# Recurrence score levels computed by 64-column halves of the TensorE array, with the diagonal joined to the first pair of levels

## The chip, the cores and the metric

The kernel runs on one core of a Trainium2 chip. The metric is the device time of one execution, in microseconds; three runs of the kernel before gave 2126.22 to 2127.8, with a median of 2127.6. A core has five engines that run side by side and meet by semaphores: TensorE (PE in the profile; its weight loads are PEld), VectorE (DVE), ScalarE (ACT), GpSimd (POOL) and SyncE (SP, which issues most DMAs). Matmul results go to PSUM, everything else lies in SBUF; both have 128 partitions.

## The reference, cut to what matters

Two layers of a decoder trunk on 512 tokens of width 1024. Each layer is a feed-forward block, a mixer and another feed-forward block. The mixer adds a gated linear recurrence (4 heads of 128 channels) and a sliding-window attention. The change lies in the recurrence:

```python
log_f = jnp.logaddexp(jnp.log(lb), jnp.log1p(-lb) + jax.nn.log_sigmoid(z))   # f = lb + (1-lb)*sigmoid(z)
k = (1.0 - lb) * jax.nn.sigmoid(-z)
...
G = jnp.cumsum(gb, axis=2)
o_inter = jnp.einsum('bhtd,bhde->bhte', qb * jnp.exp(G), state)
diff = G[:, :, :, None, :] - G[:, :, None, :, :]
decay = jnp.exp(jnp.where(causal[:, :, None], diff, -jnp.inf))
scores = jnp.einsum('bhtd,bhtsd,bhsd->bhts', qb, decay, kb)
o = o_inter + jnp.einsum('bhts,bhse->bhte', scores, vb)
```

In words: the score of query t and key s (s not after t) is the sum over channels of q[t] times k[s] times the product of the forget gates f of all tokens after s up to t. The output of a head is the score matrix times the values, normalised and gated. The reference does it in chunks of 64 tokens with a carried state; the kernel forms the whole 512 x 512 lower triangle of scores instead.

## The kernel before, in words

**Layout.** Activations lie with channels on the partitions and the 512 tokens along the free axis, in tiles `s` of 128 x 512 fp32 (61 slots). PSUM is cut into five tiles `acc` and three tiles `aux` of 128 x 512. Weights come by DMA (`w<-wall`, issued on SyncE), and each unit is split into two halves of its precision: ScalarE casts it to `whi` (L321) and VectorE subtracts to get `wlo` (L328); six such pairs are held, so a new cast waits until TensorE has done the last matmul with the pair six before it. Every projection is three matmuls per block (hi x hi, hi x lo, lo x hi; `mm3`), recorded at L115, the line of the helper `mm`. The recurrence uses plain fp32 matmuls, each of which shows as two records.

**Order of the work.** TensorE's program order is the order of the calls (manual schedule). The helper class `Order` keeps an estimated TensorE time `order.t`, to which each `mm` adds its estimated length. Side work (recurrence heads, attention blocks, transposes) is written as generators that yield a waiting time from the table `WAIT`; after the matmuls of each projection block `order.poll()` steps those that are due, at least `WAIT["rest"]` apart. So the side matmuls are placed between projection matmuls. The other engines' instructions are ordered by the scheduler of the framework; each engine runs its own list strictly in order.

**One head of the recurrence** is the generator `run` in `mixer`, which calls `recurrence_scores(q, f, kz, box)`. Its inputs are q, f and k (here `kz`), 128 channels x 512 tokens. The scores inside each chunk of 128 tokens (four chunks, tile `sd`) are built by levels b = 1, 2, 4, ..., 64: at level b the tokens are taken in groups of 2b, and the queries of the second half of a group meet the keys of its first half, both already multiplied with the gates between them and the middle of the group.

- `qa = q * f` (L943). The diagonal: four matmuls of 128 keys x 128 queries into an `aux` tile `p0`, then one VectorE product with the identity writes the whole of `sd` (L949), diagonal kept and all else zero.
- `meet(b)` (L984, L986, L988) multiplies the second-half queries and first-half keys of level b with the gate products, in place in `qa` and `kz`, and forms the products for the next level (`pr`).
- The levels are done in pairs (1,2), (4,8), (16,32). For a pair, a tile `mv` of 128 x 4 x 192 gathers the moving operand of each chunk: 64 query columns of level b (ScalarE, L995), 64 of level 2b (ScalarE, L998), and 64 of level 2b times one more gate (VectorE, L1000). After `WAIT["pair"]` four matmuls, one for each chunk, all 128 keys against 192 columns, go into two `aux` tiles `lv`. Two VectorE placements per group and `lv` tile (`place`, L972, a predicated copy with the constant `mask`) put the wanted entries into `sd`.
- The last level (64) is four matmuls of 128 keys x 64 queries, `meet(64)`, and two placements.
- Then the scores between chunks are made by larger matmuls (`s1`, `s2`; L1034 to L1043), and `run` multiplies all score blocks with the values.

In each layer heads 0 and 1 run first, beside the projections of keys and queries of attention; heads 2 and 3 run later, beside attention and the first branch projections. The score tiles, attention and the transposes share the three `aux` tiles.

**Existing matmuls with 64 stationary columns.** Attention's product with the values writes alternately to partitions 0 to 63 and 64 to 127 of one `aux` tile: `mm(po[e * HD : (e + 1) * HD, :], va[:, v0 : v0 + HD], pt[b, e], ...)` for e = 0, 1.

Of the kernel before, what the change touches and what calls it, by code (L numbers as in the profile page):

```python
# [29 lines left out]
SLOTS = 61  # L30

WAIT = dict(
    early=0.0, first=0.0, spread=2300.0, squares=1700.0, lay=34500.0, laid=770.0, normed=7600.0, final=2600.0,
    head=2600.0, diag=0.0, level=1720.0, chunks=1270.0, blocks=350.0, norm=2370.0, gate=8000.0,
    values=1200.0, scores=2000.0, exp=9000.0, shares=4500.0, turn=1900.0, turned=3000.0, rest=1200.0, lent=3500.0, apart=4000.0, block=2000.0, pair=4000.0, att0=1260.0, att1=12300.0,
)
W32, WS, AHEAD, TAIL, PLAIN, FIRST, EARLY, LATE = 4, 6, 3, 4, 4, 7, 4, 8
# [8 lines left out]
def trunk(ctx: ExitStack, tc: tile.TileContext, xin, wall, gains, lbT, hgain, sinks, c_dist, c_mask, c_ident, out):  # L46
# [25 lines left out]
    def aux():  # L72
        return ps.tile([P, S], F32, tag="aux", name=nm("aux"), bufs=3)
# [40 lines left out]
    def mm(o, lhsT, rhs, start, stop):  # L114
        nc.tensor.matmul(o, lhsT, rhs, start=start, stop=stop)  # L115
        n = 1
        for d in rhs.shape[1:]:
            n *= d
        order.t += max(n / 2.4, 27.0) * 4 if rhs.dtype == F32 else max(n / 2.4, 107.0)

    def transpose(o, src):
        nc.tensor.transpose(o, src, ident)  # L122
# [815 lines left out]
    def recurrence_scores(q, f, kz, box):  # L938

        qa = big()
        nc.vector.tensor_tensor(qa, q, f, op=ALU.mult)  # L943
        sd = big(F32, [P, TT, P])
        p0 = aux()
        for c in range(TT):
            cs = slice(c * P, (c + 1) * P)
            mm(p0[:, cs], kz[:, cs], q[:, cs], True, True)
        nc.vector.tensor_tensor(  # L949
            sd, p0.rearrange("p (c t) -> p c t", c=TT), ident.unsqueeze(1).to_broadcast([P, TT, P]), op=ALU.mult  # L950
        )
        yield WAIT["diag"]
        pr = big()
        prod, off = f, 0

        def halves(t, b):

            v = t.rearrange("p (n two b) -> p n two b", two=2, b=b)
            return v[:, :, 0, :], v[:, :, 1, :]

        def odd(t, b):
            return t.rearrange("p (c n two b) -> p c n two b", c=TT, two=2, b=b)[:, :, :, 1, :]

        def dense(t, b):
            return t.rearrange("p c (n b) -> p c n b", b=b)

        def spread(v, b):
            return v.to_broadcast([P, v.shape[1], b])

        def place(b, m, src, c):  # L970

            nc.vector.copy_predicated(  # L972
                sd.rearrange("p c (n two b) -> p c n two b", two=2, b=b)[:, c, :, 1, :],
                mask[:, m, :].rearrange("p (n b) -> p n b", b=b).unsqueeze(1).to_broadcast([P, 2, 64 // b, b]),
                dense(src, b),
            )

        def meet(b):

            nonlocal prod, off  # L980
            n = S // (2 * b)
            pv = prod.rearrange("p (n two) -> p n two", two=2)
            kv, qw = halves(kz, b)[0], halves(qa, b)[1]
            nc.vector.tensor_tensor(qw, qw, spread(pv[:, :, 0:1], b), op=ALU.mult)  # L984
            yield
            nc.vector.tensor_tensor(kv, kv, spread(pv[:, :, 1:2], b), op=ALU.mult)  # L986
            nxt = pr[:, off : off + n]
            nc.vector.tensor_tensor(nxt, pv[:, :, 0], pv[:, :, 1], op=ALU.mult)  # L988
            prod, off = nxt, off + n

        for i, b in enumerate(LEVELS[:-1:2]):


            mv = sb.tile([P, TT, 192], F32, tag="tt", name=nm("mv"), bufs=2)
            nc.scalar.copy(dense(mv[:, :, :64], b), odd(qa, b))  # L995
            first = meet(b)
            next(first)
            nc.scalar.copy(dense(mv[:, :, 64:128], 2 * b), odd(qa, 2 * b))  # L998
            way = prod.rearrange("p (c n four) -> p c n four", c=TT, four=4)[:, :, :, 1:2]
            nc.vector.tensor_tensor(  # L1000
                dense(mv[:, :, 128:], 2 * b), odd(qa, 2 * b), way.to_broadcast([P, TT, P // (4 * b), 2 * b]), op=ALU.mult
            )
            yield WAIT["pair"]
            lv = [aux()[:, :384].rearrange("p (c t) -> p c t", c=2) for _ in range(2)]
            for c in range(TT):
                mm(lv[c // 2][:, c % 2, :], kz[:, c * P : (c + 1) * P], mv[:, c, :], True, True)
            next(first, None)
            for _ in meet(2 * b):
                pass
            for j, v in enumerate(lv):  # L1010
                c = slice(2 * j, 2 * j + 2)
                place(b, 3 * i, v[:, :, :64], c)
                place(2 * b, 3 * i + 1, v[:, :, 64:128], c)
                place(2 * b, 3 * i + 2, v[:, :, 128:], c)
            yield WAIT["level"]
        b = LEVELS[-1]
        lv = aux()
        for c in range(TT):
            mm(lv[:, c * b : (c + 1) * b], kz[:, c * P : (c + 1) * P], qa[:, c * P + b : (c + 1) * P], True, True)
        for _ in meet(b):  # L1020
            pass
        v = lv[:, :256].rearrange("p (c t) -> p c t", c=TT)
        for j in range(2):
            c = slice(2 * j, 2 * j + 2)
            place(b, len(MASKS) - 1, v[:, c, :], c)
        yield WAIT["level"]

        s1 = big(F32, [P, 2, P])
        p1 = aux()
        for i, (s, t) in enumerate(((0, 1), (2, 3))):  # L1030
            mm(p1[:, i * P : (i + 1) * P], kz[:, s * P : (s + 1) * P], qa[:, t * P : (t + 1) * P], True, True)
        for s, t in ((0, 1), (2, 3)):
            ks, qt = kz[:, s * P : (s + 1) * P], qa[:, t * P : (t + 1) * P]
            nc.vector.tensor_scalar(ks, ks, prod[:, t : t + 1], None, op0=ALU.mult)  # L1034
            nc.vector.tensor_scalar(qt, qt, prod[:, s : s + 1], None, op0=ALU.mult)
        nc.scalar.copy(s1, p1[:, : 2 * P].rearrange("p (c t) -> p c t", c=2))
        yield WAIT["chunks"]

        s2 = big(F32, [P, 2, 2 * P])
        p2 = aux()  # L1040
        for s in range(2):
            mm(p2[:, s * 256 : (s + 1) * 256], kz[:, s * P : (s + 1) * P], qa[:, 256:512], True, True)
        nc.scalar.copy(s2, p2.rearrange("p (c t) -> p c t", c=2))  # L1043

        def block(s, t):
            if s == t:
                return sd[:, s, :]
            if (s, t) in ((0, 1), (2, 3)):
                return s1[:, s // 2, :]
            return s2[:, s, (t - 2) * P : (t - 1) * P]  # L1050

        box.append(block)
        yield WAIT["blocks"]
# [236 lines left out]
    nc.sync.dma_start(ident, c_ident)  # L1290
    dist = const([P, 256], "dist")
    nc.sync.dma_start(dist, c_dist)
    mask = const([P, len(MASKS), 64], "mask", I32)
    nc.sync.dma_start(mask, c_mask)
    lb_in = const([P, DEPTH, H], "lb_in")
    nc.sync.dma_start(lb_in, lbT)
    hgh = const([P, DEPTH, P], "hgh")
# [136 lines left out]
```

## Time and profile before

| what | value |
|---|---|
| runs, device us | 2127.6, 2126.22, 2127.8 (median 2127.6) |
| span of the profiled execution, first to last instruction | 2123.9 us (the runs' median lies 3.7 above it) |
| granted TensorE clock, mean over the span | 0.999 |
| TensorE busy | 2110.6 us |
| VectorE busy | 1573.4 us |
| ScalarE busy | 1119.0 us |
| predicated placements (L972) | 160, together 47.7 us busy |
| pair matmuls (`aux<-mv,s`) | 192 records, together 35.6 us busy |

"Busy" is the time in which an engine has at least one instruction in flight; the last figure of a group is the mean length of one. Instructions on one engine overlap at their ends, so a group's busy time divided by its count can be less than the mean length. In the lists in order of time the columns are start (us from the start of the span), length in us, engine, line, operation, output<-inputs, shapes and how many were merged into the row; what stands in brackets is idle time ahead and what ended it.

### The profile page before, as it was taken

Reading aid. Unit: us, or ns where it says so; the run is one execution under the profiler, and the core shown is the slowest. Engines: PE = TensorE matmul, PEld = TensorE weight load, DVE = VectorE, ACT = ScalarE, POOL = GpSimd, SP = SyncE. Lnnn points to the kernel's source line nnn. Section 1 sums busy time; section 2 is a strip of 40 time slices with the busy share of each in tenths; the row PEclk is TensorE's granted clock in tenths of the full one; section 3 lists DMA queues with packets and bytes.
Section 4 is the critical chain, followed back from the end, with each engine's and each line's share of the span. In section 5 each row is a group of like instructions: output and inputs, shape, how many; then the busy total and the mean of one; then the engine's idle time right before and its main releaser. Section 6 shows DMA issues by size and latency. Waiting matters only on the chain.

```text
span 2123.9 us, 34765 instructions
## 1 busy us (share of the span) xinstructions
PE 2110.6 (99%) x13293; PEld 1898.1 (89%) x13293; DVE 1573.4 (74%) x2793; ACT 1119.0 (53%) x1884; POOL 152.2 (7%) x180
## 2 busy tenths in 40 slices
PE   9999999999999999999999999999999999999998
PEld 8899988887888999998899998898778989999987
DVE  5877886768776777789587778767687757777884
ACT  7555555346445555556455556453554545555562
POOL 0011000000000011110001110000000000111000
PEclk9999999999999999999999999999999999999999
DMA  8677663221236357774447775632122463677751
GB/s 251 149 185 182 167 181 118 92 67 64 66 100 208 120 125 176 182 197 123 153 113 177 183 183 141 197 119 80 60 70 60 124 194 110 149 180 182 185 158 51
DMA packets 146870, 298.48 MB, mean 141 GB/s; under 512 B 15664, under 2 KB 73488, under 8 KB 146704
## 3 DMA queue, kind: packets, MB, share of 16 engines
q1 hardware_dynamic: 121216, 228.31, 32.7%
q0 software_dynamic: 25344, 67.91, 18.6%
q8 instruction: 104, 1.70, 0.3%
q14 instruction: 62, 0.51, 0.1%
q10 hardware_dynamic: 144, 0.05, 0.0%
HBM read 213.58 MB, written 14.73 MB: 107 GB/s over the span
## 4 chain that ended last, share of the span: by engine, by line
PE 75%; DVE 7%; ACT 3%; issue 1%; DMA 1%; SPq 0%; ACTq 0%; DVEq 0%
PE acc L115 55%; PE aux L115 19%; DVE s L398 1%; PE aux L122 1%; ACT whi L321 1%; DVE wlo L283 1%; DMA w<-wall 1%; DVE wlo L328 1%; PE acc L122 1%; ACT s L397 1%; DVE tt L265 0%; DVE w L264 0%; DVE s L273 0%; DVE w L274 0%; ACT whi L278 0%
## 5 line engine op out<-in xcount | busy, mean ns | idle before, releaser
L115 PE MATMUL acc<-s,whi 128*128 128x256 f32 (+1 forms) x4968 | 1068.8, 312 | 0.7 <-DVE s L901 0.7
L115 PEld LDWEIGHTS acc<-s,whi 128*128 128x128 f32 x4968 | 810.1, 191 | 48.7 <-issue 3.7
L115 PE MATMUL acc<-s,wlo 128*128 128x256 f32 (+1 forms) x2484 | 770.2, 310 | 0.1
L115 PEld LDWEIGHTS acc<-s,wlo 128*128 128x128 f32 x2484 | 474.1, 191 | 26.0 <-DVE wlo L328 0.4
L321 ACT CAST whi<-w 128x1024 fp32r<-128x1024 f32 (+1 forms) x341 | 316.6, 947 | 242.0 <-PE aux L115 100.2
L115 PE MATMUL acc<-whi,s 128*128 128x512 f32 x1264 | 414.5, 394 | 0.0
L321 ACT CAST whi<-tt 128x1024 fp32r<-128x1024 f32 x154 | 161.4, 1048 | 337.7 <-DVE tt L315 199.5
L328 DVE TENSOR_TENSOR wlo<-w,whi 128x1024 fp32r<-128x1024 f32 (+1 forms) x181 | 218.5, 1216 | 135.3 <-ACT whi L321 131.6
L115 PEld LDWEIGHTS acc<-whi,s 128*128 128x128 f32 x1264 | 237.1, 188 | 55.7 <-issue 3.2
L328 DVE TENSOR_TENSOR wlo<-tt,whi 128x1024 fp32r<-128x1024 f32 x154 | 188.1, 1222 | 101.6 <-ACT whi L321 101.6
L326 POOL DMA_DIRECT2D wlo<-w x160 | 138.2, 865 | 1723.5 <-ACT wlo L325 1363.1
L115 PE MATMUL acc<-wlo,s 128*128 128x512 f32 x632 | 246.7, 390 | 1.2 <-DVE wlo L283 1.2
L115 PE MATMUL aux<-s,whi 128*128 128x256 f32 x1232 | 225.1, 283 | 0.0
L115 PE MATMUL aux<-whi,s 128*128 128x512 f32 x592 | 196.7, 390 | 0.0
L115 PEld LDWEIGHTS aux<-s,whi 128*128 128x128 f32 x1232 | 192.2, 192 | 0.0
L115 PE MATMUL aux<-s,wlo 128*128 128x256 f32 x616 | 174.3, 283 | 0.0
L115 PEld LDWEIGHTS acc<-wlo,s 128*128 128x128 f32 x632 | 118.8, 188 | 25.5 <-DVE wlo L283 2.4
L115 PEld LDWEIGHTS aux<-whi,s 128*128 128x128 f32 x592 | 111.2, 188 | 22.9
L325 ACT ACTIVATE wlo<-w 128x1024 fp32r<-128x1024 f32 (+1 forms) x160 | 129.8, 844 | 0.0
L397 ACT CAST s<-s 128x512 fp32r<-128x512 f32 (+1 forms) x164 | 88.4, 580 | 75.8 <-DVE s L456 72.2
L115 PEld LDWEIGHTS aux<-s,wlo 128*128 128x128 f32 x616 | 118.3, 192 | 0.0
L115 PE MATMUL aux<-wlo,s 128*128 128x512 f32 x296 | 115.2, 389 | 0.0
(182 smaller groups left out, 2189.1 us busy)
## 6 DMA issues: line engine op xcount, KB each, us to landing
w<-wall SPq DMA_DIRECT2D x267, 512.0 KB, 3.7
wlo<-w POOLq DMA_DIRECT2D x83, 512.0 KB, 5.5
w<-wall SPq DMA_DIRECT2D x288, 128.0 KB, 3.4
wlo<-w POOLq DMA_DIRECT2D x77, 256.0 KB, 3.3
x_d<-s SPq DMA_DIRECT2D x48, 256.0 KB, 2.1
s<-x_d SPq DMA_DIRECT2D x48, 256.0 KB, 5.5
w<-wall SPq DMA_DIRECT2D x34, 256.0 KB, 3.2
s<-wall SPq DMA_DIRECT2D x64, 128.0 KB, 3.7
```

The source lines that it names most:

```text
L115: nc.tensor.matmul(o, lhsT, rhs, start=start, stop=stop)
L122: nc.tensor.transpose(o, src, ident)
L283: nc.vector.tensor_tensor(it.lo[:, h[c]], w[c], it.hi[:, h[c]].bitcast(F32), op=ALU.subtract)
L321: i = nc.scalar.copy(it.hi[:, c], w[:, c])
L325: nc.scalar.mul(it.lo[:, c], w[:, c], -1.0)
L326: nc.gpsimd.dma_start(it.lo[:, c].bitcast(F32), w[:, c], accum_op=ALU.add)
L328: nc.vector.tensor_tensor(it.lo[:, c], w[:, c], it.hi[:, c].bitcast(F32), op=ALU.subtract)
L397: nc.scalar.copy(hi, src)
L398: nc.vector.tensor_tensor(lo, src, hi.bitcast(F32), op=ALU.subtract)
```

## The change

The recurrence inside the chunks of 128 is cut into halves of 64 tokens, eight in all:

- For the three pairs of levels each half's 64 keys are the stationary operand (64 columns of the TensorE array) and meet only that half's own queries. The results of even halves go to partitions 0 to 63 of the PSUM tile, those of odd halves to partitions 64 to 127, in alternation. A half has 32 columns per group, so `mv` has 96 columns per half instead of 192 per chunk, and four chunks fit into one `aux` tile for the second and third pair.
- The diagonal is no longer a step of its own. The first pair carries 64 more columns per half, a copy of q made by ScalarE, so 160 columns per half, in two `aux` tiles; four VectorE products with the identity (one for each half and tile, on 64 partitions) write the diagonal blocks of `sd`. GpSimd sets to zero the quarter of `sd` that no level writes.
- `place` works on 64 partitions at a time, two instructions (one per half) for each group: on 64 x 64 entries in the first pair (two chunks at a time), on 64 x 128 in the others (four chunks).
- The last level uses only the first 64 keys of each chunk against the last 64 queries, into partitions 0 to 63, and ScalarE copies the result into `sd`; no placement.
- `Order` counts an fp32 matmul with 64 stationary columns and under 256 moving columns half as long. The mask is smaller and is loaded by two DMAs. Two entries of `WAIT` go (`diag`, and the unused `early`).

```diff
@@ -116,7 +116,10 @@
         n = 1
         for d in rhs.shape[1:]:
             n *= d
-        order.t += max(n / 2.4, 27.0) * 4 if rhs.dtype == F32 else max(n / 2.4, 107.0)
+        if rhs.dtype == F32:
+            order.t += max(n / 2.4, 27.0) * (2 if lhsT.shape[1] == 64 and n < 256 else 4)
+        else:
+            order.t += max(n / 2.4, 107.0)
 
     def transpose(o, src):
         nc.tensor.transpose(o, src, ident)
@@ -942,14 +945,7 @@
         qa = big()
         nc.vector.tensor_tensor(qa, q, f, op=ALU.mult)
         sd = big(F32, [P, TT, P])
-        p0 = aux()
-        for c in range(TT):
-            cs = slice(c * P, (c + 1) * P)
-            mm(p0[:, cs], kz[:, cs], q[:, cs], True, True)
-        nc.vector.tensor_tensor(
-            sd, p0.rearrange("p (c t) -> p c t", c=TT), ident.unsqueeze(1).to_broadcast([P, TT, P]), op=ALU.mult
-        )
-        yield WAIT["diag"]
+        nc.gpsimd.memset(sd[64:, :, :64], 0.0)
         pr = big()
         prod, off = f, 0
 
@@ -959,21 +955,24 @@
             return v[:, :, 0, :], v[:, :, 1, :]
 
         def odd(t, b):
-            return t.rearrange("p (c n two b) -> p c n two b", c=TT, two=2, b=b)[:, :, :, 1, :]
+            return t.rearrange("p (x n two b) -> p x n two b", x=2 * TT, two=2, b=b)[:, :, :, 1, :]
 
         def dense(t, b):
-            return t.rearrange("p c (n b) -> p c n b", b=b)
+            return t.rearrange("p x (n b) -> p x n b", b=b)
 
         def spread(v, b):
             return v.to_broadcast([P, v.shape[1], b])
 
-        def place(b, m, src, c):
-
-            nc.vector.copy_predicated(
-                sd.rearrange("p c (n two b) -> p c n two b", two=2, b=b)[:, c, :, 1, :],
-                mask[:, m, :].rearrange("p (n b) -> p n b", b=b).unsqueeze(1).to_broadcast([P, 2, 64 // b, b]),
-                dense(src, b),
-            )
+        def place(b, m, lv, g, c):
+
+            n = c.stop - c.start
+            for h in range(2):
+                r = slice(64 * h, 64 * h + 64)
+                nc.vector.copy_predicated(
+                    sd[r].rearrange("p c (x n two b) -> p c x n two b", x=2, two=2, b=b)[:, c, h, :, 1, :],
+                    mask[r, m, :].rearrange("p (n b) -> p n b", b=b).unsqueeze(1).to_broadcast([64, n, 32 // b, b]),
+                    dense(lv[r, :, g * 32 : g * 32 + 32], b),
+                )
 
         def meet(b):
 
@@ -991,38 +990,46 @@
         for i, b in enumerate(LEVELS[:-1:2]):
 
 
-            mv = sb.tile([P, TT, 192], F32, tag="tt", name=nm("mv"), bufs=2)
-            nc.scalar.copy(dense(mv[:, :, :64], b), odd(qa, b))
+            w = 96 if i else 160
+            cs = [slice(0, 4)] if i else [slice(0, 2), slice(2, 4)]
+            mv = sb.tile([P, 2 * TT, w], F32, tag="tt", name=nm("mv"), bufs=2)
+            if i == 0:
+                nc.scalar.copy(mv[:, :, 96:], q.rearrange("p (x t) -> p x t", x=2 * TT))
+            nc.scalar.copy(dense(mv[:, :, :32], b), odd(qa, b))
             first = meet(b)
             next(first)
-            nc.scalar.copy(dense(mv[:, :, 64:128], 2 * b), odd(qa, 2 * b))
-            way = prod.rearrange("p (c n four) -> p c n four", c=TT, four=4)[:, :, :, 1:2]
+            nc.scalar.copy(dense(mv[:, :, 32:64], 2 * b), odd(qa, 2 * b))
+            way = prod.rearrange("p (x n four) -> p x n four", x=2 * TT, four=4)[:, :, :, 1:2]
             nc.vector.tensor_tensor(
-                dense(mv[:, :, 128:], 2 * b), odd(qa, 2 * b), way.to_broadcast([P, TT, P // (4 * b), 2 * b]), op=ALU.mult
+                dense(mv[:, :, 64:96], 2 * b), odd(qa, 2 * b), way.to_broadcast([P, 2 * TT, 16 // b, 2 * b]), op=ALU.mult
             )
             yield WAIT["pair"]
-            lv = [aux()[:, :384].rearrange("p (c t) -> p c t", c=2) for _ in range(2)]
-            for c in range(TT):
-                mm(lv[c // 2][:, c % 2, :], kz[:, c * P : (c + 1) * P], mv[:, c, :], True, True)
+            lv = [aux()[:, : (c.stop - c.start) * w].rearrange("p (c t) -> p c t", t=w) for c in cs]
+            for c, v in zip(cs, lv):
+                for x in range(2 * c.start, 2 * c.stop):
+                    h = slice(64 * (x % 2), 64 * (x % 2) + 64)
+                    mm(v[h, x // 2 - c.start, :], kz[:, x * 64 : x * 64 + 64], mv[:, x, :], True, True)
             next(first, None)
             for _ in meet(2 * b):
                 pass
-            for j, v in enumerate(lv):
-                c = slice(2 * j, 2 * j + 2)
-                place(b, 3 * i, v[:, :, :64], c)
-                place(2 * b, 3 * i + 1, v[:, :, 64:128], c)
-                place(2 * b, 3 * i + 2, v[:, :, 128:], c)
+            for c, v in zip(cs, lv):
+                if i == 0:
+                    for h in range(2):
+                        r = slice(64 * h, 64 * h + 64)
+                        nc.vector.tensor_tensor(
+                            sd[r, c, r], v[r, :, 96:], ident[r, r].unsqueeze(1).to_broadcast([64, 2, 64]), op=ALU.mult
+                        )
+                place(b, 3 * i, v, 0, c)
+                place(2 * b, 3 * i + 1, v, 1, c)
+                place(2 * b, 3 * i + 2, v, 2, c)
             yield WAIT["level"]
         b = LEVELS[-1]
         lv = aux()
         for c in range(TT):
-            mm(lv[:, c * b : (c + 1) * b], kz[:, c * P : (c + 1) * P], qa[:, c * P + b : (c + 1) * P], True, True)
+            mm(lv[:b, c * b : (c + 1) * b], kz[:, c * P : c * P + b], qa[:, c * P + b : (c + 1) * P], True, True)
         for _ in meet(b):
             pass
-        v = lv[:, :256].rearrange("p (c t) -> p c t", c=TT)
-        for j in range(2):
-            c = slice(2 * j, 2 * j + 2)
-            place(b, len(MASKS) - 1, v[:, c, :], c)
+        nc.scalar.copy(sd[:b, :, b:], lv[:b, : TT * b].rearrange("p (c t) -> p c t", c=TT))
         yield WAIT["level"]
 
         s1 = big(F32, [P, 2, P])
@@ -1290,8 +1297,9 @@
     nc.sync.dma_start(ident, c_ident)
     dist = const([P, 256], "dist")
     nc.sync.dma_start(dist, c_dist)
-    mask = const([P, len(MASKS), 64], "mask", I32)
-    nc.sync.dma_start(mask, c_mask)
+    mask = const([P, len(MASKS) - 1, 32], "mask", I32)
+    for h in range(2):
+        nc.sync.dma_start(mask[64 * h : 64 * h + 64], c_mask[64 * h : 64 * h + 64, :-1, 32 * h : 32 * h + 32])
     lb_in = const([P, DEPTH, H], "lb_in")
     nc.sync.dma_start(lb_in, lbT)
     hgh = const([P, DEPTH, P], "hgh")
```

More of the change, by code (lines that the diff above doesn't have):

```diff
@@ L32 @@
 WAIT = dict(
-    early=0.0, first=0.0, spread=2300.0, squares=1700.0, lay=34500.0, laid=770.0, normed=7600.0, final=2600.0,
-    head=2600.0, diag=0.0, level=1720.0, chunks=1270.0, blocks=350.0, norm=2370.0, gate=8000.0,
+    first=0.0, spread=2300.0, squares=1700.0, lay=34500.0, laid=770.0, normed=7600.0, final=2600.0,
+    head=2600.0, level=1720.0, chunks=1270.0, blocks=350.0, norm=2370.0, gate=8000.0,
     values=1200.0, scores=2000.0, exp=9000.0, shares=4500.0, turn=1900.0, turned=3000.0, rest=1200.0, lent=3500.0, apart=4000.0, block=2000.0, pair=4000.0, att0=1260.0, att1=12300.0,
```

## The prediction

> **What bounds the kernel now.** I read the page first (busy time by engine), then who waited for whom on TensorE, then the busy time in the two stretches where heads 0 and 1 of each layer are computed, then the chain of work that ended last inside the first of them.
>
> ```profile
> span 2123.9 us, 34765 instructions
> PE 2110.6 (99%) x13293; PEld 1898.1 (89%) x13293; DVE 1573.4 (74%) x2793; ACT 1119.0 (53%) x1884; POOL 152.2 (7%) x180
> ...
> PE aux L115 <- DVE s L972: 3.2, 2, 1.6
> ...
> 385.00:435.00 50.00, 48.40 (x249) 41.46 (x249) 40.34 (x116) 16.64 (x31) 0.00 (x0) 1.00 0.23 79
> 1440.00:1490.00 50.00, 48.40 (x250) 41.35 (x249) 37.90 (x115) 16.06 (x29) 0.00 (x0) 1.00 0.20 64
> ```
>
> TensorE (PE) is busy 2110.6 of 2123.9 us, so the time is TensorE's work plus its few waits; matmul time taken away is time won unless a wait replaces it. The only wait inside the recurrence is for the placements (L972): 1.6 us, once in each layer. The last two lines warn: in these 50 us (columns: length, PE, PEld, VectorE, ScalarE, GpSimd, clock, DMA) VectorE (DVE) is busy 40.34 and 37.90. It has about 10 us to spare in the place that the change touches.
>
> The runs shown have a median of 2127.6, which is 3.7 above the span of the profiled execution; I leave those 3.7 as they are and add the sum to 2127.6.
>
> ```profile
> 387.50 0.89 PE aux L115 x8
> ...
> 395.96 1.06 ACT whi L321
> ...
> 397.05 1.23 DVE wlo L328
> 398.27 0.60 DVE s L401
> ...
> 400.68 0.93 DVE s L972 x3
> 401.61 0.14 issue
> 401.74 0.89 PE aux L115 x4
> 402.63 6.14 PE acc L115 x27
> 408.78 1.30 PE aux L115 x8
> 410.08 1.40 PE acc L115 x6
> ...
> 424.32 0.84 PE aux L115 x8
> 425.16 1.44 PE acc L115 x6
> ...
> 467.48 1.01 PE aux L115 x4
> 468.49 1.59 PE acc L115 x6
> ...
> 483.23 1.87 PE aux L115 x8
> ```
>
> This is the chain in order of time (start, length, what). The four fp32 matmuls of a block are eight records: the diagonal takes 0.89, a pair block 1.30, the last level 0.84 plus 0.05 more in what follows it (1.44 instead of 1.39 to 1.40 for six projection matmuls). One projection matmul is 6.14/27 = 0.227. The last three lines are attention's product with the values, the only existing matmuls with 64 stationary columns, written to alternating halves of the output partitions: four records 1.01, eight 1.87.
>
> **The change, part by part.**
>
> *TensorE, removed.* Per head 0.89 + 3 x 1.30 + 0.89 = 5.68 us.
>
> *TensorE, added.* From 1.01 and 1.87, two more pairs of records cost 0.86, so a pair of 64-column matmuls over 512 columns (two pairs of records) costs 0.86: 1.68 ns per column, and both halves together cost what one full-width matmul costs (1.30/4/192 = 1.69 ns per column). That is the overlap on which the change rests. What is left of the 1.01 is 0.15, and the six matmuls behind take 1.59 instead of 1.40: 0.34 is paid for each visit to the halves. New per head: first block 4 pairs x 160 columns = 1.08; second and third 4 x 96 = 0.65 each; last level 4 single halves x 64 = 0.43; four visits 1.36; together 4.17. Saved: 1.51 a head, 12.1 in eight heads.
>
> No row shows pairs as short as 96 columns. The lower end is the rate above (a part that costs still less has no reason). The upper end is the last level of now: 64 columns in 0.89/4 = 0.22 a matmul, though 1.69 x 64 is 0.11, so something other than the columns sets it.
>
> ```profile
> 424.16 1.00 PE L115 MATMUL aux<-s,s 128*128 128x64 f32 x8
> ...
> 423.93 1.09 PEld L115 LDWEIGHTS aux<-s,s 128*128 128x128 f32 x8
> ...
> 483.16 1.94 PE L115 MATMUL aux<-s,s 128*64 128x512 f32 x8
> ...
> 483.15 0.20 PEld L115 LDWEIGHTS aux<-s,s 128*64 128x64 f32 x4 [0.36 <-issue]
> ```
>
> It is the weight load: eight loads of 128 columns fill 1.09 beside eight matmuls. In the half-array block four loads of 64 columns are started within 0.20 of each other, beside the matmuls, so a load for a half is at most half as dear, and I take the column rate. At 0.22 a pair (and a last-level matmul) the saving would fall by 0.95 a head to 4.5 in all. [...]
>
> *VectorE.* Gone per head: one diagonal product (128x512) and two placements of the last level, whose copy goes to ScalarE. New: four diagonal products on 64 partitions, twelve placements of 64x64 in the first pair instead of six of 128x128, and twelve of 64x128 in place of twelve of 128x128 later.
>
> ```profile
> 402.05 0.43 DVE L972 COPY_PREDICATED s<-mask,aux 128x128 f32<-128x128 int32 x1
> ...
> 403.55 1.90 DVE L972 COPY_PREDICATED s<-mask,aux 128x128 f32<-128x128 int32 x6
> ...
> 424.64 0.89 DVE L972 COPY_PREDICATED s<-mask,aux 128x128 f32<-128x128 int32 x4
> ...
> 514.49 0.28 DVE L1193 TENSOR_TENSOR s<-aux,s 128x128 fp32r<-128x128 f32 x1
> 513.89 0.88 DVE L1193 TENSOR_TENSOR s<-aux,s 128x128 fp32r<-128x128 f32 x4
> ...
> 405.94 0.76 DVE L1000 TENSOR_TENSOR mv<-s,s 128x256 f32<-128x256 f32 x2
> ```
>
> Neighbours overlap at their ends. Six first-pair placements take 1.90, the last one 0.43 of it: 0.29 each. Later levels: (0.89 - 0.29)/3 = 0.20. A product of 128 elements: (0.88 - 0.28)/3 = 0.20. A 256-element product 0.34. No row shows an operation on 64 partitions or a first-pair placement of half the length. Lower end: 0.19, by elements and overlapped; upper end: 0.43, the whole length of one, with nothing overlapped. I take 0.29 for the new first-pair placements, the rate of the same instruction at the same level, because each of them still waits for the one two before it (same half, same data), as those six did; and 0.20 for the rest.
>
> *What this does to TensorE's waits.* I go through the built program's order with these prices. Both programs are the same until 387.34, the start of the diagonal.
>
> ```profile
> 387.34 1.05 PE L115 MATMUL aux<-s,s 128*128 128x128 f32 x8
> ...
> 406.88 1.05 ACT L321 CAST whi<-w 128x1024 fp32r<-128x1024 f32 x1
> 406.59 0.40 ACT L998 COPY mv<-s 128x256 f32<-128x256 f32 x1
> ```
>
> (a) 21 projection matmuls follow instead of the diagonal, so head 0's first block comes at 392.1 (396.6 now). Its operand is ready just then (weight cast until 389.7, two copies, VectorE behind a weight split until 392.0): at most 0.1. It ends at 393.5; head 1's follows at 394.9 and wants a fourth score tile from three buffers at 395.6. VectorE can start at 393.65, since its key update overwrites what the block reads: three updates and a small product 1.2, two diagonal products 0.4, six placements 1.74, so 397.0. **Wait 1.5.**
>
> (b) TensorE goes on until 397.95, then 27 matmuls: 404.1, head 0's second block. VectorE before its operand: second tile of head 0 2.14; head 1's updates 1.56; its two tiles 2 x 2.14; an attention split 0.60; two query updates 0.67; the operand 0.34; 0.15 to signal: 406.75. **Wait 2.65.** From there until the end of heads 0 and 1 VectorE is 0.9 or more ahead.
>
> (c) Heads 2 and 3: between head 3's first block and head 2's last level stand 3.73 us of other TensorE work and blocks of 1.4 and 1.0; VectorE has head 3's two tiles and seven updates to do: **wait 1.55.**
>
> Sum 5.7 a layer instead of 1.74 (the 1.60 idle and 0.14 of issue in the chain): 7.9 given back in two layers. The two copies added on ScalarE (0.58 and 0.4 a head) lie in its idle time (16.64 busy of 50), the first inside the 392.0 above. GpSimd's clearing of a quarter of the tile has no queue behind it (0.00 busy in both stretches). The mask's two loads instead of one lie at the start, long before use.
>
> **Sum: -12.1 + 7.9 = -4.2, so 2123.4.**
>
> **Rivals.**
>
> *Cheap placements.* If half the elements cost half the columns' time (0.185), (a) becomes 0.9 and (c) 0.3. (b) does not vanish: ScalarE has the cast of the next weights (1.05), freed by TensorE two matmuls ahead of the block, and only then the operand's copy (0.40), so about 1.25. 2.45 a layer: 2127.6 - 12.1 + 1.4 = 2116.9. For it: the trace's other prices do go with elements. Against: the 0.29.
>
> *All half-partition work unoverlapped.* Operations take turns between partitions 0 to 63 and 64 to 127; if each waits until the one before has ended, products cost 0.28, later placements 0.29, and the waits are about 1.8, 3.3 and 2.05: 7.15 a layer, 2127.6 - 12.1 + 10.8 = 2126.3. No row speaks on it, as no VectorE instruction here starts at partition 64. [...]
>
> *Slower: first-pair placements at full length.* If they take 0.43 each, unoverlapped and no shorter for half the data, (a), (b) and (c) grow by 36 x 0.14 = 5.0 a layer to 10.7: 2127.6 - 12.1 + 17.9 = 2133.4. It turns to a loss where the waits exceed 7.8 a layer, at 0.35 per placement. For it: 0.43 alone at 402.05. Against: six of them ran in 1.90.
>
> That the halves do not run side by side at 96 and 160 columns would cost 1.08 + 1.3 = 2.38 a head more, some 7 us slower than now; the pairs at 483.16 speak against it, and it goes with the slower case.
>
> **How the numbers follow.** Forecast 0.38 (2119.5 to 2127 of its own: weight-load floor above, a VectorE order that falls out better below), cheap 0.27, unoverlapped 0.15, slower 0.20. A measurement can tell about 0.2%, 4.3 us, from no change. Faster by more: all of the cheap case and somewhat over half of the forecast, 0.50. Within: the rest of the forecast and most of the unoverlapped case, 0.28. Slower: 0.22. The range reaches from 2115 (cheap, with (b) hidden too) to 2132, just short of the dearest price.
>
> **What the profile after would show.** The matmul groups with 128*64 and 160 or 96 columns should come in pairs of equal starts; blocks of about 1.4, 1.0, 1.0 and 0.8 on the chain. Placements of 64x64 at 0.29 from start to start confirm the price; at 0.19 the cheap case holds, above 0.35 the slow one. TensorE's waits for the placements and for the second operand should sum to about 4.2 in heads 0 and 1 of each layer. The prediction is wrong at its root if pairs take turns, or if a wait opens elsewhere, above all on weight splits queued behind the placements.

## The result and the profile after

The changed kernel takes 2139.09 us (median of four runs, 2138.71 to 2139.65), the kernel before 2126.91 us beside it: a ratio of 1.0056, 95% interval 1.0041 to 1.007. It is about 12 us slower; 2123.4 us were predicted, in a range up to 2132. The prediction was wrong.

First the page of the changed kernel, busy time by engine:

```profile
span 2137.4 us, 35103 instructions
...
PE 2110.2 (99%) x13421; PEld 1880.2 (88%) x13421; DVE 1595.5 (75%) x2849; ACT 1125.0 (53%) x1900; POOL 154.6 (7%) x188
```

TensorE has less to multiply and is busy for as long as before (2110.6). VectorE is busy 22.1 us longer. The view of who waited for whom on TensorE (total, times, longest), its rows that the change touches:

```profile
PE aux L115 <- DVE mv L1003: 6.3, 2, 3.9
PE aux L115 <- DVE s L985: 5.5, 2, 2.8
PE aux L115 <- DVE s L971: 3.4, 2, 1.7
...
PE aux L115 <- DVE s L1042: 1.1, 2, 0.7
```

Once a layer TensorE waits for a score tile (L971), for head 0's second operand (L1003), for the last key update of head 2 (L985), and a little for the step after it (L1042): 16.3 us in all, against 3.2 before. Next the busy time by stretches; the first and third lie in heads 0 and 1 of the two layers, the others in heads 2 and 3, and the clock is the number after POOL:

```profile
400.00:420.00 20.00, 17.66 (x89) 13.55 (x88) 18.28 (x57) 6.50 (x13) 0.00 (x0) 0.83 0.00 1
540.00:560.00 20.00, 17.11 (x103) 12.64 (x101) 17.37 (x55) 5.01 (x9) 0.00 (x0) 0.83 0.09 27
1465.00:1485.00 20.00, 18.07 (x123) 13.58 (x123) 18.11 (x58) 5.32 (x11) 0.00 (x0) 0.91 0.08 27
1605.00:1625.00 20.00, 16.56 (x106) 13.12 (x105) 16.65 (x48) 6.28 (x11) 0.00 (x0) 0.91 0.26 80
```

VectorE is busy 16.65 to 18.28 of 20 us here. Over the whole 50 us of heads 0 and 1 it is busy more than 45 us in each layer, where the kernel before had 40.34 and 37.90:

```profile
385.00:435.00 50.00, 45.97 (x267) 35.39 (x265) 45.66 (x130) 17.92 (x35) 0.00 (x0) 0.93 0.18 59
1440.00:1490.00 50.00, 44.37 (x273) 34.64 (x273) 45.36 (x127) 19.72 (x36) 0.00 (x0) 0.97 0.18 61
```

And the granted clock, 1.00 throughout the recurrence before, falls. In the trace's clock records it is half for stretches of 3.413 us: two such stretches in each of the first two windows, one in each of the others, 20.5 us at half clock in all. A mean of 0.83 over 20 us is 6.8 us at half.

The chain of work that ended last, in heads 0 and 1 of the first layer (start, length, what):

```profile
395.92 0.31 DVE s L1019
...
396.24 0.30 DVE s L971
396.55 0.02 issue
396.56 0.31 DVE s L971
396.88 0.02 issue
396.90 0.30 DVE s L971
...
407.25 0.30 DVE s L971
407.57 0.69 DVE s L404
408.26 0.67 DVE s L983 x2
408.93 0.35 DVE mv L1003
409.27 0.14 issue
409.41 1.01 PE aux L115 x16
410.42 2.86 PE acc L115 x6
...
420.52 0.81 PE aux L115 x16
421.33 1.58 PE acc L115 x6
...
425.31 0.61 PE aux L115 x8
425.92 1.59 PE acc L115 x6
```

Before, VectorE held this chain only between 397.05 and 401.61. Now it runs on VectorE up to 409.27, for more than 13 us: mostly placement behind placement, each starting 0.32 to 0.34 after the one before, with key and query updates and products between them. Then TensorE takes over, and six projection matmuls cost 2.86 instead of 1.40: that is the half clock.

### The profile page after: what moved, and what is told of

Same layout as the page of the kernel before. It is cut to its first block, busy times and chain, and to the rows that moved or that the text cites. A ratio compares the mean times of both kernels' runs of the same rounds, so it can differ in the third digit from the quotient of the medians.

```text
span 2137.4 us, 35103 instructions
## 1 busy us (share of the span) xinstructions
PE 2110.2 (99%) x13421; PEld 1880.2 (88%) x13421; DVE 1595.5 (75%) x2849; ACT 1125.0 (53%) x1900; POOL 154.6 (7%) x188
## 4 chain that ended last, share of the span: by engine, by line
PE 76%; DVE 12%; ACT 5%; issue 3%; DMA 2%; SPq 1%; ACTq 0%; DVEq 0%; POOLq 0%
PE acc L115 55%; PE aux L115 18%; ACT whi L324 2%; DVE s L971 2%; DMA w<-wall 2%; DVE s L401 1%; PE aux L125 1%; DVE wlo L331 1%; DVE wlo L286 1%; ACT s L400 1%; SPq L241 1%; PE acc L125 1%; ACT m L894 1%; ACT wlo L328 1%; DVE tt L268 0%
```

## The experiments

My theory after this profile had two parts. VectorE's placements change their start partition (0 or 64) from one instruction to the next and so lose their overlap; and the waits that this makes on TensorE drop its clock, which costs again. Rivals: half-partition instructions are slow wherever they start; the new order is at fault; the clock drop has another cause, or costs nothing by itself. "Starts" below counts, in VectorE's instruction list, how often the start partition changes, in the first pair and in the later two.

| kernel | us | ratio to before, 95% | changes of start, first pair / later |
|---|---|---|---|
| changed kernel | 2139.09 | 1.0056 (1.0041 to 1.007) | 128 / 96 |
| low_start | 2115.91 | 0.9951 (0.9935 to 0.9968) | 0 / 0 |
| whole_place | 2113.83 | 0.994 (0.9925 to 0.9955) | 0 / 0 |
| idle_filled | 2138.92 | 1.0058 (1.0043 to 1.0073) | 128 / 96 |
| no_placements | 2110.58 | 0.9925 (0.991 to 0.9939) | 0 / 0 |
| high_start | 2118.26 | 0.9959 (0.9944 to 0.9974) | 36 / 52 |
| idle_filled2 | 2139.09 | 1.0061 (1.0043 to 1.0079) | 128 / 96 |
| pair_later | 2137.43 | 1.0055 (1.0039 to 1.0071) | 224 in all |
| last_level_only | 2126.54 | 1.0 (0.999 to 1.001) | 0 / 0 |
| by_half | 2126.85 | 1.0001 (0.9991 to 1.001) | 76 / 96 |
| one_half_first | 2120.9 | 0.9973 (0.9963 to 0.9983) | 0 / 0 |
| by_half_low | 2115.65 | 0.9947 (0.9931 to 0.9964) | 0 / 0 |
| first_pair_changes | 2133.41 | 1.0034 (1.0021 to 1.0047) | 128 / 0 |

### low_start and high_start: is it the start?

```diff
 low_start, in place and in the diagonal products:
-r = slice(64 * h, 64 * h + 64)
+r = slice(0, 64)
 high_start:
+r = slice(64, 128)
```

> Part left out: the placements and diagonal products of the odd halves read and write partitions 0 to 63 (at the columns of their own half), and GpSimd clears the whole upper half of the score tile; count, shapes and order of VectorE's and TensorE's instructions are those of the changed kernel. Only the start partition differs. Theory (an instruction that starts on the other half of the partitions is held until the one before has ended): from start to start 0.20 to 0.24 us between neighbouring placements instead of 0.31 to 0.335, TensorE's waits in heads 0 to 2 about 7 to 9 us less in all, fewer half-clock windows, 2124 us (2119 to 2129). Rival (half the partitions or half the elements cost 0.3 us wherever they lie): starts 0.3 apart as before, 2139 (2137 to 2141).

> Part left out: the placements and diagonal products of the even halves read and write partitions 64 to 127 (at the columns of their own half), and GpSimd clears the whole lower half of the score tile; the order and shapes on VectorE and TensorE are those of the changed kernel. The counterpart of the run with all starts at partition 0. Theory (what costs is that the start changes from one instruction to the next): neighbouring placements 0.18 to 0.22 us apart, with a few tenths a block lost where a full-partition update stands between; 2117 us (2115 to 2122). Rival (an instruction that starts at partition 64 is itself slow, 0.3 us): 56 placements and products a layer more start there than in the changed kernel, so no faster than it, 2139 or more.

Measured 2115.91 and 2118.26. With every start at 0 the time falls by 23.2 us, more than the theory asked for; with every start at 64 by 20.8, so partition 64 is not slow in itself. The same stretch of VectorE in time order, the changed kernel first:

```profile
396.24 1.93 DVE L971 COPY_PREDICATED s<-mask,aux 64x64 f32<-64x64 int32 x6
398.20 0.61 DVE L1019 TENSOR_TENSOR s<-aux,ident 64x128 f32<-64x128 f32 x2
```

low_start:

```profile
394.92 1.07 DVE L971 COPY_PREDICATED s<-mask,aux 64x64 f32<-64x64 int32 x6
395.84 0.47 DVE L1019 TENSOR_TENSOR s<-aux,ident 64x128 f32<-64x128 f32 x2
```

Six placements take 1.93 with changing starts and 1.07 with one start. The groups (busy time, mean ns of one), in the changed kernel:

```profile
L971 DVE COPY_PREDICATED s<-mask,aux 64x64 f32<-64x64 int32 x96 | 28.6, 298 | 2.7
L971 DVE COPY_PREDICATED s<-mask,aux 64x128 f32<-64x128 int32 x96 | 28.3, 295 | 2.3
```

and in low_start:

```profile
L971 DVE COPY_PREDICATED s<-mask,aux 64x128 f32<-64x128 int32 x96 | 21.1, 280 | 0.0
L971 DVE COPY_PREDICATED s<-mask,aux 64x64 f32<-64x64 int32 x96 | 17.7, 291 | 0.0
```

The length of one hardly differs (298 and 291 ns); busy time over count does: 28.6/96 = 0.30 against 17.7/96 = 0.18. In the changed kernel the busy time is count times length, so nothing overlaps. That a change of the start is what takes the overlap away is shown: count, order and shapes of VectorE's instructions are the same in these runs, and high_start, with every start at 64, overlaps too (six placements in 1.11 us at 395.40). The prediction's rival of unoverlapped half-partition work is borne out; the price is 0.32 from start to start in place of 0.18 to 0.22. For the whole kernel VectorE's busy time differs by 26.9 us (1595.5 against 1568.6) and the time by 23.2: here nearly all of what VectorE loses stands on the path.

### no_placements: TensorE's saving alone

The diff drops the loop with `place` and the diagonal products and clears all of `sd` on GpSimd.

> Part left out: all placements and diagonal products; GpSimd clears the whole score tile instead, and TensorE's matmuls stay. What TensorE alone saves, with nothing queued on VectorE. Theory (TensorE's part was priced right at 12 us, the waits took it): 2114 us (2111 to 2117), waits only for the second operand, 1.3 us at most. Rival (the blocks by halves save less than 12 us): 2120 or more with as few waits.

Measured 2110.58, 16.3 less than before and 3 below the expected 2114. The 3.2 us of waits of the kernel before are gone with the placements, which leaves 13.1 for the blocks (TensorE's busy time falls by 12.5, from 2110.6 to 2098.1); 12.1 were predicted. I had left those 3.2 out of the expectation.

### whole_place: one placement for both halves

```diff
-for h in range(2):
-    r = slice(64 * h, 64 * h + 64)
-    nc.vector.copy_predicated(sd[r]...[:, c, h, :, 1, :], mask[r, m, :]..., dense(lv[r, ...], b))
+nc.vector.copy_predicated(sd...[:, c, 0, :, 1, :], mask[:, m, :]..., dense(lv[:, ...], b))
...
+nc.scalar.copy(sd[64:, :, 64:], sd[64:, :, :64])      # after the third pair
+nc.gpsimd.memset(sd[64:, :, :64], 0.0)
```

> TensorE as in the changed kernel; each placement and diagonal product covers all 128 partitions at once (both halves lie at the columns of the lower one, and ScalarE moves the upper half's result to its own columns at the end of the third pair, 0.4 us a head). 12 placements and 2 products a head instead of 24 and 4, none starts at partition 64. Theory (VectorE's time by halves makes the waits, the waits make the half clock): waits at most 2 us a layer, clock full, and the TensorE saving of 12 us comes through: 2115 us (2112 to 2119). Rival (the order is at fault: the diagonal joined to the first pair and the blocks earlier after each other): the waits for the second operand and the last level stay at 2 us or more each, 2128 (2124 to 2134).

Measured 2113.83: the theory's number, and faster than both kernels. The groups of this kernel:

```profile
L968 DVE COPY_PREDICATED s<-mask,aux 128x128 f32<-128x128 int32 x48 | 14.0, 291 | 0.1
L968 DVE COPY_PREDICATED s<-mask,aux 128x64 f32<-128x64 int32 x48 | 11.7, 297 | 0.2
L1014 DVE TENSOR_TENSOR s<-aux,own 128x128 f32<-128x128 f32 x16 | 4.4, 283 | 0.0
```

An instruction on 128 partitions is as long as one on 64 (297 against 298 ns), so half the count does the same work: 25.7 us busy on placements against 56.9. Its wait for the placements is 1.0 us in two times. The order of TensorE's blocks is that of the changed kernel, so the rival that blames the order falls.

### idle_filled and idle_filled2: is the half clock a cost of its own?

```diff
+def idle(t, n):
+    for _ in range(n):
+        nc.tensor.matmul(t[:, 384:], ident, ident, start=True, stop=True)
...
+if head == 0 and i == 1: idle(full[0], 10)   # 16 in idle_filled2; 6 and 10 at the other two waits
```

> The changed kernel with 26 more fp32 matmuls of 128x128 (identity on identity, 0.26 us each, results unused) in each layer, put where TensorE waits: 6 ahead of head 1's second score tile of the first block, 10 ahead of head 0's second block, 10 ahead of head 2's last level. They add 13.5 us of TensorE work in all and no other engine gets anything. Theory (each wait of 1.7 us or more drops the clock to half for 3.41 us, and that costs about 1.2 us each, six times): the mean granted clock comes back from 0.994 to 0.998 or more and the time falls in spite of the added work, to 2133 us (2130 to 2136). Rival (the clock drops for another reason, as the matmuls on half the array): half-clock windows stay and the time is 2139 to 2142.

> The first filling left a wait of 1.7 us ahead of head 0's second block and moved one of 2.5 us to head 2's step after the last level, so half-clock windows stayed. Here 16 instead of 10 idle matmuls at the former, and 8 at the latter: 40 idle matmuls a layer, 20.8 us of added TensorE work. Theory (the waits drop the clock, and what the slow matmuls behind a wait lose is on the path, 1.2 to 1.7 us for each of the two waits after which TensorE isn't caught by VectorE again): no half-clock window in the two stretches, 2134 us (2131 to 2137). Rival (VectorE's chain sets the end of each stretch, and a slow TensorE only shortens the next wait): 2138 to 2140 with the clock at full.

Measured 2138.92 and 2139.09. The first was inconclusive: three of the six half-clock stretches stayed, because part of the waits stayed. The second is clear; its rows for the same four stretches:

```profile
400.00:420.00 20.00, 19.47 (x138) 16.02 (x136) 19.19 (x61) 5.69 (x11) 0.00 (x0) 1.00 0.09 28
540.00:560.00 20.00, 18.92 (x141) 15.68 (x141) 19.11 (x58) 5.11 (x10) 0.00 (x0) 1.00 0.17 53
1465.00:1485.00 20.00, 18.66 (x142) 14.22 (x141) 19.25 (x59) 6.44 (x13) 0.00 (x0) 1.00 0.25 79
1605.00:1625.00 20.00, 18.95 (x141) 16.09 (x140) 16.42 (x47) 6.27 (x11) 0.00 (x0) 1.00 0.25 80
```

The clock is full in all four, and the time is that of the changed kernel. Half of my theory falls here: the clock drop follows the waits (1.00 in all four rows, with no wait over 0.6 us left in the recurrence), but giving the clock back buys nothing in the whole time. Who waited for whom on TensorE, idle_filled2:

```profile
PE aux L115 <- DVE s L985: 3.5, 10, 0.5
...
PE aux L115 <- DVE s L1053: 1.3, 2, 0.6
...
PE aux L115 <- ACT mv L1005: 0.8, 2, 0.4
...
PE aux L115 <- DVE s L971: 0.3, 2, 0.2
```

Ten waits for L985 stand where the changed kernel has two, eight of them in heads 0 and 1: as soon as TensorE runs at full clock behind the second operand, it catches up with VectorE and waits again. The account agrees: in the changed kernel TensorE loses 16.3 us to waits and half of 20.5 to the clock, 26.5; here it loses 20.8 to idle matmuls (80 at about 0.26) and 5.9 to these waits, 26.7. The chain of idle_filled2 says the same more directly. In the first layer it stays on VectorE through the two heads' levels, up to the score blocks between chunks:

```profile
430.21 0.35 DVE s L985
430.56 0.04 issue
430.60 0.71 PE aux L115 x4
```

The next such block starts at 432.71, against 433.37 in the changed kernel: the two half-clock stretches there, which cost TensorE 3.4 us, are worth 0.66 of time. VectorE sets the length of the stretch, however TensorE spends the difference.

### pair_later: more time between the blocks

```diff
-pair=4000.0
+pair=6500.0
```

> The changed kernel with the estimated waiting time ahead of each pair block raised from 4.0 to 6.5 us, so that more projection matmuls lie ahead of each block; nothing is computed otherwise. Theory (VectorE is short of time only for some 20 us with two heads at once; with more matmuls between, its backlog is worked off under TensorE's work): waits of head 0's second block under 1 us, 2122 us (2117 to 2129). Rival (VectorE's backlog only moves, to the steps behind): 2136 to 2141.

Measured 2137.43: the rival. The waits for head 0's second operand are gone from the view, and others are there instead:

```profile
PE aux L115 <- DVE s L1042: 6.4, 4, 2.0
PE aux L115 <- DVE s L971: 5.4, 2, 2.7
```

The wait for a score tile has grown from 3.4 to 5.4 us and that at L1042 from 1.1 to 6.4. The clock records show one half-clock stretch of 3.413 us in the recurrence here, where the changed kernel has six; that the time falls by only 1.7 us also speaks against the clock as a cost of its own.

### by_half, by_half_low and first_pair_changes: how many changes, and where

by_half does all of the even half of a tile before the odd half; by_half_low is by_half with `r = slice(0, 64)`; first_pair_changes is the changed kernel with `r = slice(64 * h, 64 * h + 64) if m < 3 else slice(0, 64)` in `place`.

> The changed kernel with the calls in another order: for each score tile first all products and placements of the even half, then all of the odd half, in place of even and odd in turn. Work, shapes and count are the same. The scheduler mixes the two score tiles and the other updates in between, so that VectorE's start partition changes 172 times in its instruction list instead of 224 times (0 in the run with all starts at partition 0, 88 in the one with all at 64). Theory (each change costs the overlap of two neighbours, and in these stretches VectorE's time is the kernel's time): between the run at 0 and the changed kernel lie 23.2 us for 224 changes, 0.104 us each, so 172 changes give 2115.9 + 17.8 = 2134 us (2130 to 2137). Rival (the number of instructions on half the partitions counts, not the changes): 2139 (2138 to 2141).

> Part left out as in the run with all starts at 0: the odd halves' placements and products use partitions 0 to 63; the call order is that of the run by halves. By halves came out at 2126.85, 7 us below what 52 changes fewer should bring by the mean price. Theory (the changes alone make the difference to the changed kernel, at a price that grows once VectorE's spare time in a stretch is used up): without changes the order is worth nothing, 2116 us (2114 to 2118). Rival (the order itself helps, since TensorE's wanted updates come earlier in VectorE's list): 4 us less than with the old order and starts at 0, 2112.

> Part left out: the odd halves' placements of the second and third pair use partitions 0 to 63; the first pair's placements and products are as in the changed kernel, and so are order and shapes. VectorE's start changes 128 times instead of 224. Theory (convex price: spare time first, then the full price, by the points 88 changes 2118.3, 172 changes 2126.9): 2122 us (2119 to 2125). Rival (each change costs the same 0.104 us): 2129; rival (the first pair's changes, ahead of the score tile and the second operand, carry nearly all): 2134 or more.

Measured 2126.85, 2115.65 and 2133.41. A constant price per change is wrong (2134 and 2129 by it), and so is the convex curve over the count (2122 for first_pair_changes). by_half_low shows that the order by itself does nothing. The place of a change matters. The 52 changes that by_half saves all lie in the first pair and bring 12.2 us (0.235 each); the 96 changes of the later pairs cost 5.7 us (0.06 each, from first_pair_changes to the changed kernel). But two fixed prices do not fit either. If the later changes cost 5.7 in by_half too, its 76 changes in the first pair cost only 5.3 (0.07 each), and all 88 changes of high_start cost 2.4, although VectorE is busy 10.1 us longer there than in low_start (1578.7). So the first changes are cheap and further ones dear. That VectorE's spare time takes the first ones is argued; no run tests it by itself. The waits of first_pair_changes:

```profile
PE aux L115 <- DVE mv L1003: 7.9, 2, 3.9
PE aux L115 <- DVE s L985: 4.6, 2, 2.3
PE aux L115 <- DVE s L971: 3.4, 2, 1.7
```

With the later pairs overlapping again these waits sum to 15.9, as much as the three rows of the changed kernel (15.2): the changes in the first pair are enough to make them. The first pair's placements stand ahead of the fourth score tile and of the next operand. Why a change there costs 0.235 when it makes an instruction only some 0.14 longer isn't settled; VectorE's busy time differs by only 6.8 us between by_half and the changed kernel.

### last_level_only and one_half_first: TensorE's part

last_level_only is the kernel before with the changed last level. one_half_first is whole_place with the order of the matmuls in a tile changed:

```diff
-for x in range(2 * c.start, 2 * c.stop):
+for x in [*range(2 * c.start, 2 * c.stop, 2), *range(2 * c.start + 1, 2 * c.stop, 2)]:
```

> The kernel before with one part of the change alone: the last level with the first 64 keys of each chunk (64 stationary columns into partitions 0 to 63) and ScalarE's copy in place of two placements. By the measured block (0.84 in the changed kernel against 0.89) 0.05 us a head, 0.4 in all, and two placements of 0.2 us less on VectorE at a place with no wait: 2126.4 us (2125 to 2127.5), not to be told from no change. Rival (the two placements were what the wait for the placements hung on): 2.5 to 3.2 us less, 2124.

> The kernel with placements over all 128 partitions (2113.8 us), with one thing changed on TensorE: in each score tile the matmuls of all even halves come first, then those of all odd halves, in place of even and odd in turn. VectorE's list is the same. Theory (two halves run side by side only as neighbours; what the change saves on TensorE hangs on it): 1.08 + 2 x 0.65 = 2.38 us more a head less the one neighbouring pair in the middle of each tile, so 13 to 19 us more, 2130 us (2126 to 2134). Rival (the halves cost half the columns whatever the order): 2113 to 2115.

last_level_only measured 2126.54 against 2126.64: no difference, as expected. one_half_first measured 2120.9, 7.1 us more than whole_place where 13 to 19 were expected. The groups of whole_place:

```profile
L115 PE MATMUL aux<-mv,s 128*64 128x96 f32 x256 | 14.1, 253 | 0.0
...
L115 PE MATMUL aux<-mv,s 128*64 128x160 f32 x128 | 10.9, 307 | 1.0 <-DVE s L968 1.0
```

and of one_half_first:

```profile
L115 PE MATMUL aux<-mv,s 128*64 128x96 f32 x256 | 20.2, 252 | 0.0
...
L115 PE MATMUL aux<-mv,s 128*64 128x160 f32 x128 | 11.2, 309 | 0.9 <-DVE s L968 0.9
```

The tiles with eight halves lose 6.1 us, those with four halves 0.3. So the saving does hang on two halves running side by side, but they need not be direct neighbours: in the records of a four-half tile the odd half's matmuls still start 0.01 to 0.06 us after the even ones, and in an eight-half tile the first odd matmul starts 0.39 us after the first even one, with even ones still to start. The records do not name the half; this is read from the starts, which form two interleaved rows. My expectation had taken only direct neighbours to overlap.

## Why the prediction was wrong, step by step

- **TensorE removed and added: right.** Blocks of about 1.4, 1.0, 1.0 and 0.8 were predicted. The chain has 0.81 at 420.52 with 1.58 behind it instead of 1.40, so 0.99, and 0.61 at 425.31 with 1.59, so 0.80. The saving was 12.1 by the sum and 13.1 by no_placements. The pairs run side by side, and so do their loads: a 96-column block has 16 loads of 0.145 on average, 2.3 one after the other, and those of the block at 420.52 all lie within 0.69 us from 420.45, beside its matmuls, so it can be at 0.81.
- **VectorE's prices: this step failed.** "I take 0.29 for the new first-pair placements [...] and 0.20 for the rest": 0.32 from start to start for all 56 instructions of a pair of heads, whatever their number of elements. The 0.29 and 0.20 were overlapped rates of instructions that all start at partition 0. On such starts the 0.29 would even have been too dear (0.18 in low_start) and the 0.20 about right (0.22). The new thing in the diff was the start at 64, and no row of before showed one; it was put into a rival instead of into the price.
- **The waits: right places, too small.** (a) 1.5 was predicted, 1.7 came; (b) 2.65, came 2.3 and 3.9; (c) 1.55, came 2.8 in both layers; the wait at L1042 (0.4 and 0.7) was not foreseen. Together 16.3 instead of 11.4. In heads 0 and 1 of the first layer the sum is 4.0, close to the 4.2 that the prediction gave as its sign; that is no success, since VectorE's lateness shows there as half clock instead.
- **"From there until the end of heads 0 and 1 VectorE is 0.9 or more ahead": wrong, and the larger part of the miss.** The changed kernel shows no wait there, but only because TensorE ran at half clock. With the clock full in idle_filled2 waits stand there, and the chain stays on VectorE up to 430.56. I priced three waits at the places where VectorE would be late first, and let the stretch end on TensorE's time; in fact VectorE, with half-partition work at its full length, sets the stretch up to its end. The gap of 15.7 us to 2123.4 is 4.9 of larger waits and 10.2 of slow clock, both of which are VectorE's lateness; 0.6 is left over, as long as the prediction's starting point (2127.6) and its 12.1 of saving are kept.
- **The clock** wasn't in the prediction at all. As an account it is the largest missing term; as a cause it is next to none, 0.66 of the 3.4 us in the one stretch followed here and nothing in the whole time.
- **The rivals.** *Cheap placements* gave 2116.9, and low_start, which has those prices, 2115.91: the sum was sound with the right price. *Unoverlapped* had the right condition (in the changed kernel nothing overlaps: 28.6 us busy for 96 placements of 0.298) and gave 2126.3, 12.8 too low, for it priced at 0.28 and 0.29 and kept the same three waits. The *slower* case had the right side and a time (2133.4) 5.7 off by another mechanism: only the first pair unoverlapped, at 0.43 each. Measured, the later placements are unoverlapped too, and one takes 0.30, not 0.43. The reason that the prediction gave for a dear first pair, that each placement waits for the one two before it, is refuted, since low_start has the same data dependences and 0.18. That the first pair's price decides was right (first_pair_changes: 17.5 of the 23.2 us). Its turning point in waits, 7.8 a layer, was passed with 8.15.
- **The joined diagonal, ScalarE's copies, GpSimd's clearing, the mask: right at nothing.** whole_place keeps all four, with one copy more, and no wait for them shows.

## What to carry to other kernels

Before splitting work into partition halves, look at what the engine behind the matmuls does with the halves: an instruction over all partitions cost as much as one over half of them here (297 against 298 ns), and alternating starts took away the overlap of neighbours (0.32 us from start to start in place of 0.18 to 0.22), so lay both halves at the same columns and move one of them once at the end. When two engines come near each other's limit in a stretch, sum the whole queue of the second engine to the stretch's end instead of pricing the waits that are seen first. A slow clock or a wait on the waiting engine can be the same lost time under two names (26.5 us of waits and half clock in the changed kernel, 26.7 of idle matmuls and waits in idle_filled2); give one of them back and see whether the other grows.

## What the runs showed of the hardware

- VectorE: with changing start partitions 0.32 us from start to start for 64 and 128 elements alike; with one start 0.18 and 0.22 (0, low_start) or 0.19 and 0.23 (64, high_start, by busy time over count). The dependence of a placement on the one two before it did not prevent the overlap in low_start (six placements in 1.07 us).
- In the changed kernel TensorE's clock went to half after five of the six longer waits (1.7, 2.3, 2.8 twice, 3.9 us), for 3.413 us each time and for 3.413 twice in a row in heads 2 and 3 of the first layer. After the same wait of 1.7 us in the second layer it stayed full, and in pair_later it stayed full after one of two waits of 2.7, so the length of a wait alone does not decide. In the kernel before a wait of 1.6 us left the clock full in each layer (1.00 in both stretches of 50 us).
- TensorE: in one_half_first matmuls for the other half of the columns started ahead of matmuls that stand before them in the program, over at least three records (0.39 us after the first one in an eight-half tile).
